# A first norm whose factor is applied to the results of the products, not to their input

## The chip, the cores and the metric

One core of one Trainium2 chip runs the whole program. The metric is the time of one execution on the device, in microseconds (us); the kernel before has a median of 1431.68 us over three runs.

## The reference

One step of a two-layer streaming encoder for 640 frames: 512 of a new stream and 8 x 16 of running streams, 1024 channels each, float32. What matters here is the beginning of layer 0:

```python
def rms_norm(x, g):
    y = xf * lax.rsqrt(jnp.mean(xf * xf, axis=-1, keepdims=True) + EPS)
    return (y * g).astype(x.dtype)

def conv_module(h, hist, g, w_pw1, b_pw1, w_dw, b_dw, ln_g, ln_b, w_pw2, b_pw2):
    a, gate = jnp.split(rms_norm(h, g) @ w_pw1 + b_pw1, 2, axis=-1)
    glu = a * jax.nn.sigmoid(gate)
    full = jnp.concatenate([hist, glu], axis=1)
    y = depthwise_conv(full, w_dw) + b_dw          # 31 taps per channel, causal
    y = jax.nn.silu(layer_norm(y, ln_g, ln_b))
    return h + y @ w_pw2 + b_pw2, full[:, -30:]
```

After it come a feed-forward block, attention, a second feed-forward block and a last norm. They take up the span from about 236 us on and are not touched.

## The kernel before

**Layout.** Channels lie on the 128 partitions: tile `h` is 128 x 8 x 640, eight channel tiles `k` by 640 frames. The frames go in two groups, `g` = 0 and 1, of 320 (`GS`; group 0 holds the 128 frames of the running streams). A float32 product is made of three TensorE products (`mm3`): each operand is split into a rounded part and a rest (`xh`, `xl` for the input, `whi`, `wlo` for weights), and high x high, high x low and low x high are added in PSUM. A split is one activation on ScalarE and one subtraction on VectorE.

**First norm and first products.** `rms(g)` squares the eight tiles of `h` (ScalarE, for group 0 three of them on VectorE), adds them, sums over the partitions with a 128 x 1 product (`colmean`), takes the power -1/2 on GpSimd, and spreads the factor over the partitions with a 128 x 128 product into PSUM (`spread`). Only then `n = h * gain * factor` can be computed (L309), and `xsplit` splits `n` (L190, L192). `glu(c, g)` makes channel tile `c` (0 to 7) of the projection: two PSUM tiles, value and gate, of 24 products each (eight `k` by three). ScalarE reads both with scale and bias (`tanh` at L814, a copy at L817), VectorE multiplies them into `gall` (L823, L830; one half of the channels' `gp`/`gs` views). These two are called the gate below.

**Convolution.** The 31 taps run on three engines: for most channel tiles as products on TensorE (`conv_pe`, L923, after a trip through DRAM that shifts the frames), for channel tiles 0 and 3 of the long stream as scaled copies on ScalarE (`cvt`, L876, four buffers) that GpSimd adds (`ca`, L879), and for the rest as 155 multiply-adds on VectorE (L866, L869: 62 of 512 frames and 93 of 128). When all of `y` is there, `conv_ln(0)` sums it on VectorE (`acc`, L233) and TensorE takes the mean (L243).

**Order.** `PLAN` lists the steps; `a`, `b`, `c`, `C` to `F` are projections. Each step is recorded, and a scheduler lays out each engine's queue by priorities. An engine works its queue off strictly in that order. The PSUM pool `mm0` has four tiles of 128 x 512. Input and weights are read through the queue of SyncE (SP), `vecs` (gains, biases: tile `vec`; tap weights: tile `dwv`) through that of ScalarE. `conv_load` (L890, GpSimd) multiplies `dwv` into a diagonal form for `conv_pe`. `warm(n)` issues products without a use.

Of the kernel before, what the change touches and what calls it, by code (L numbers as in the profile page):

```python
# [15 lines left out]
P = 128  # L16
# [26 lines left out]
WARM_END = 5  # L43
HP = 2000
# [3 lines left out]
PL1 = (0, 2, 0, 0, 0, 0, 0, 0)  # L48
# [7 lines left out]
SSQ = 'avavavaa'  # L56
# [16 lines left out]
WARM = 30, 9, 5, 0  # L73
LNO = ((0, 1, 4, 5, 6, 3, 2, 7), (0, 1, 4, 2, 3, 5, 6, 7))
PLAN = ("a0 y x1 b0 b1 q0 dp1s0 c2 ds1p2 D3 C4 S3 q3 C5 E6 u S4 A4 F6 u k ds2 B4 E7 e S5 A5 F7 f k k k S6 A6 "
# [10 lines left out]
def tile_trunk(ctx, tc, xT, vecs, hist, w_pw1, w_pw2, w_in0, w_out0, w_os0, w_in1, w_out1, w_os1,  # L86
# [36 lines left out]
    load_x(0)  # L123
    vec = cst.tile([P, V_N], F32, name="vec", tag="vec")
    nc.scalar.dma_start(vec, vecs[:, 0:V_N])
    ident = cst.tile([P, P], F32, name="ident", tag="ident")
# [25 lines left out]
    def wsplit(src, k, n, parts=1, pool=0, cuts=1, gains=None, late=False, ties=()):  # L152
        raw = wp.tile([P, 2048], F32, tag="raw", name=nm("raw"))
# [18 lines left out]
        def split():  # L172
            with tc.high_priority(offset=HP):
                for i in range(cuts):
                    a, b = sz * i // cuts, sz * (i + 1) // cuts
                    tie = ties[i] if isinstance(ties, list) else ties
                    with behind(*tie):
                        nc.scalar.activation(out=hi[:, a:b], in_=raw[:, a:b], func=AF.Copy)
                    c = b - (b - a) * pool // 4
                    for eng, a, b in ((nc.vector, a, c), (nc.gpsimd, c, b)):  # L180
                        if a < b:
                            with behind(*tie):
                                eng.tensor_tensor(out=lo[:, a:b], in0=raw[:, a:b],
                                                  in1=hi[:, a:b].bitcast(F32), op=ALU.subtract)
            return hi, lo
# [36 lines left out]
    def colmean(st, pieces, n, cut, tag, eng=nc.gpsimd, accp=None, late=(KT, None)):  # L222
# [17 lines left out]
        for k, f in enumerate(srcs):  # L240
            s = f()
            for t, a in enumerate(tiles(n)):
                mean_end[0] = nc.tensor.matmul(st[:, 512 + t * w + k:513 + t * w + k], s[:, a:a + P],  # L243
                                               onec, start=True, stop=True).ins
# [8 lines left out]
    norm_spread, cover = [None], []  # L253
# [44 lines left out]
    def rms(g, gain, engs=SQ, cut=CUT, eng=nc.gpsimd, hold=None, hook=None):  # L298
        n = gr[g][1]
        bc, _ = rstd_bc([hp(g, k) for k in range(KT)], n, engs, cut, None, eng,  # L300
                        accp=hold and hold(), hook=hook)
        xh, xl = new_xs(g)
        if WARM[2 + g]:
            with behind(norm_spread[0]):
                warm(WARM[2 + g])
        for k in range(KT):
            t = hold() if hold and k < 2 else tp.tile([P, tw[0]], F32, tag="n1", name=nm("n1"),
                                                       bufs=NB1)
            norm_end["n"].append(nc.vector.scalar_tensor_tensor(  # L309
                out=t[:, :n], in0=hp(g, k), scalar=col(gain, k), in1=bc, op0=ALU.mult,  # L310
                op1=ALU.mult).ins)
            xsplit(t[:, :n], xh[:, k, :], xl[:, k, :])
        return xh, xl, None, None
# [464 lines left out]
    pws[1] = wsplit(w_pw1[1], 16, P, cuts=4, pool=PL1[1],  # L778
                    ties=(norm_end["sq"], norm_end["n"][3], norm_end["pow"]))
    load_hist(0, 2)  # L780
    nc.scalar.dma_start(dwv, vecs[:, V_N:])
# [7 lines left out]
    def glu(c, g, wh, wl, mid=None):  # L789
        glu_(c, g, wh, wl, mid)  # L790
        if g == 0:
            nc.sync.dma_start(convs_out[:, c], gs[:, c])

    def glu_(c, g, wh, wl, mid):
        n = gr[g][1]
        ps = []
        for ab in range(2):
            pt = mmt()
            def some(ks):
                return mm3(pt[:, :n], [(wh[:, (ab * 8 + k) * P:(ab * 8 + k + 1) * P],  # L800
                                        wl[:, (ab * 8 + k) * P:(ab * 8 + k + 1) * P])
                                       for k in ks], xk(xs[g], ks), ks[0] == 0, ks[-1] == KT - 1)

            if mid and ab:
                mid(lambda: some(range(0, 4)).ins)
                with tc.issue_after(norm_spread[0]):
                    some(range(4, KT))
            else:
                some(range(KT))
            ps.append(pt[:, :n])  # L810
        with tc.high_priority(offset=HP):
            cover.clear()
            t = tp.tile([P, tw[0]], F32, tag="t1", name=nm("t1"))
            glu_end[0] = nc.scalar.activation(out=t[:, :n], in_=ps[1], func=AF.Tanh, scale=0.5,  # L814
                                              bias=hb1[:, KT + c:KT + c + 1]).ins
# [12 lines left out]
            o = HIST + g * NH - NB * SB * g  # L828
            with behind(*tie):
                gate_end[0] = nc.vector.scalar_tensor_tensor(  # L830
                    out=gp[:, c, o:o + n - ns], in0=t[:, ns:n], scalar=1.0, in1=a[:, ns:n],
                    op0=ALU.add, op1=ALU.mult).ins

# [207 lines left out]
    def step(op, arg):  # L1041
# [11 lines left out]
        elif op == "y":  # L1053
            load_x(1)
        elif op == "x":
            def mid(some):
                def hook():
                    with tc.issue_after(mean_end[0]):
                        cover[:] = [some()]

                with behind(norm_end["xh"][2], norm_end["pow"]):
                    xs[1] = rms(1, V_NCONV, SSQ1, 8, hold=w4t, hook=hook)
            glu(1, 0, *pws[1], mid=mid)
# [813 lines left out]
```

## Time and profile before

| what | us |
|---|---|
| median of 3 runs (lowest, highest) | 1431.68 (1431.62, 1432.91) |
| the profiled execution | 1431.78 |
| its span in the profile | 1430.0 |
| TensorE busy in the span | 1416.8 |
| VectorE, ScalarE, GpSimd busy | 1113.5, 746.9, 278.4 |

In the profile each row of a timeline has start, duration, engine, line, operation, output<-inputs with shapes and a count, and in brackets the idle time before it and what ended that. PE is TensorE, DVE VectorE, ACT ScalarE, POOL GpSimd. A TensorE instruction on float32 without the split (`warm`, sums, spreads) stands there as two.

### The profile page before, as it was taken

To read this page: it belongs to the slowest core of one execution; us is meant where nothing else is said; L and a number is where in the kernel's file an instruction comes from. 1 tells how busy PE (TensorE), PEld (TensorE's weight loads), DVE (VectorE), ACT (ScalarE), POOL (GpSimd) and SP (SyncE) were. 2 spreads that over 40 slices of the span, in tenths; PEclk is the share of its full clock that TensorE was granted. 3 is DMA by queue.
4 is the path that set the end of the run, shared out by engine and by line. 5 is a ranking of instruction groups with operands and counts; after the bars stand their busy time and mean duration, and the time that the engine had idled before them with its cause. 6 is when DMAs were issued, how large, how long until landed. Compare 5 with 4: busy or idle time off the path is not lost.

```text
span 1430.0 us, 28700 instructions
## 1 busy us (share of the span) xinstructions
PE 1416.8 (99%) x11076; PEld 1364.0 (95%) x11076; DVE 1113.5 (78%) x2490; ACT 746.9 (52%) x1633; POOL 278.4 (19%) x335
## 2 busy tenths in 40 slices
PE   9999999999999999999999999999999999999998
PEld 9998799999999999999998998888999999999998
DVE  7799867898888888765666757667898798798765
ACT  5666554554653554545654554544564564464453
POOL 5699121011111110112111111110011111111101
PEclk9999999999999999999999999999999999999999
DMA  7267424154644644524456555561244544554522
GB/s 248 91 176 187 123 84 143 32 122 122 169 107 121 148 115 117 139 89 174 165 185 205 187 179 173 181 218 51 60 108 118 147 125 110 145 131 109 135 72 74
DMA packets 93722, 192.62 MB, mean 135 GB/s; under 512 B 15121, under 2 KB 45585, under 8 KB 90129
## 3 DMA queue, kind: packets, MB, share of 16 engines
q1 hardware_dynamic: 79216, 160.59, 36.0%
q0 software_dynamic: 13504, 29.37, 10.5%
q8 instruction: 87, 1.43, 0.4%
q10 hardware_dynamic: 864, 0.83, 0.2%
q14 instruction: 51, 0.41, 0.1%
HBM read 179.14 MB, written 11.61 MB: 133 GB/s over the span
## 4 chain that ended last, share of the span: by engine, by line
PE 93%; DVE 4%; ACT 1%; issue 1%; DMA 1%; POOL 0%; DVEq 0%; ACTq 0%; POOLq 0%
PE mm L451 52%; PE mm L1311 11%; PE mm L202 6%; PE mm L204 6%; PE mm L203 6%; PE mm L923 3%; PE w L1311 2%; PE am L1484 1%; PE am L1556 1%; PE am L1500 1%; PE w L1455 1%; PE w L1518 1%; PE w L243 1%; PE mm L149 1%; PE w L257 1%
## 5 line engine op out<-in xcount | busy, mean ns | idle before, releaser
L451 PE MATMUL mm<-XH,whi 128*128 128x320 f32 x896 | 275.9, 310 | 1.0 <-ACT t L463 0.7
L451 PE MATMUL mm<-XH,wlo 128*128 128x320 f32 x896 | 276.2, 309 | 0.0
L451 PE MATMUL mm<-XL,whi 128*128 128x320 f32 x896 | 274.7, 309 | 0.0
L375 ACT ACTIVATE whi<-raw 128x512 fp32r<-128x512 f32 (+2 forms) x280 | 167.5, 613 | 148.4 <-PE mm L451 91.9
L376 DVE TENSOR_TENSOR wlo<-raw,whi 128x512 fp32r<-128x512 f32 (+2 forms) x280 | 183.8, 667 | 29.8 <-ACT whi L375 29.2
L451 PE MATMUL mm<-hid,whi 128*128 128x320 f32 x732 | 170.9, 310 | 0.0
L451 PEld LDWEIGHTS mm<-XH,whi 128*128 128x128 f32 x896 | 167.7, 188 | 2.8 <-ACT t L463 1.5
L451 PEld LDWEIGHTS mm<-XH,wlo 128*128 128x128 f32 x896 | 168.2, 188 | 0.0
L451 PEld LDWEIGHTS mm<-XL,whi 128*128 128x128 f32 x896 | 167.7, 188 | 0.0
L202 PE MATMUL mm<-xh,whi 128*128 128x320 f32 (+2 forms) x416 | 128.8, 312 | 0.5 <-DVE h L733 0.4
L203 PE MATMUL mm<-xh,wlo 128*128 128x320 f32 (+2 forms) x416 | 128.0, 309 | 0.0
L204 PE MATMUL mm<-xl,whi 128*128 128x320 f32 (+2 forms) x416 | 125.5, 310 | 1.0 <-DVE xl L192 1.0
L451 PEld LDWEIGHTS mm<-hid,whi 128*128 128x128 f32 x732 | 124.8, 188 | 1.5 <-DVE h L602 0.9
L451 PE MATMUL mm<-hid,wlo 128*128 128x320 f32 x366 | 113.0, 309 | 0.0
L451 PE MATMUL mm<-XH,shi 128*128 128x320 f32 x344 | 106.2, 310 | 1.2 <-DVE h L1588 0.7
L451 PE MATMUL mm<-XH,slo 128*128 128x320 f32 x344 | 106.0, 308 | 0.0
L602 DVE TENSOR_TENSOR h<-h,mm 128x320 f32<-128x320 f32 x168 | 79.1, 482 | 34.2 <-PE mm L451 34.2
L451 PE MATMUL mm<-XL,shi 128*128 128x320 f32 x344 | 105.6, 308 | 0.0
L375 ACT ACTIVATE shi<-raw 128x512 fp32r<-128x512 f32 (+1 forms) x114 | 66.4, 588 | 59.6 <-PE mm L451 31.6
L879 POOL TENSOR_TENSOR ca<-ca,cvt 128x512 f32<-128x512 f32 x60 | 89.5, 1492 | 17.3 <-ACT cvt L876 11.1
L428 POOL DMA_DIRECT2D s<-in_w_in x38 | 22.0, 578 | 309.1 <-ACT shi L375 67.3
L376 DVE TENSOR_TENSOR slo<-raw,shi 128x512 fp32r<-128x512 f32 (+1 forms) x114 | 72.0, 636 | 12.4 <-ACT shi L375 12.0
(337 smaller groups left out, 3663.1 us busy)
## 6 DMA issues: line engine op xcount, KB each, us to landing
raw<-in_w_in SPq DMA_DIRECT2D x152, 256.0 KB
s<-in_w_in POOLq DMA_DIRECT2D x76, 256.0 KB, 4.3
raw<-in_w_os SPq DMA_DIRECT2D x96, 192.0 KB
cache<-in_ck SPq DMA_DIRECT2D x32, 512.0 KB
cache<-in_cv SPq DMA_DIRECT2D x32, 512.0 KB
raw<-in_w_pw SPq DMA_DIRECT2D x11, 1024.0 KB
s<-in_w_os POOLq DMA_DIRECT2D x48, 192.0 KB, 3.6
raw<-in_w_kq SPq DMA_DIRECT2D x8, 1024.0 KB
```

Of the source, the lines that this page charges most:

```text
L149: end = nc.tensor.matmul(pt[:, 0:P], ident, ident, start=True, stop=True)
L202: nc.tensor.matmul(ps, wh, xh, start=(first and i == 0), stop=False)
L203: nc.tensor.matmul(ps, wl, xh, start=False, stop=False)
L204: end = nc.tensor.matmul(ps, wh, xl, start=False, stop=(stop and i == last))
L375: put_end[1] = nc.scalar.activation(out=hi, in_=src, func=AF.Copy).ins
L376: put_end[0] = nc.vector.tensor_tensor(out=lo, in0=src, in1=hi.bitcast(F32), op=sub).ins
L428: nc.gpsimd.dma_start(s1, src[:, 2 * n:3 * n])
L451: last = nc.tensor.matmul(pt, wt, v, start=(first and k == i == 0), stop=(k == n - 1 and i == 2), skip_group_check=True)
L602: hadd[i, u] = [nc.vector.tensor_tensor(out=hv, in0=hv, in1=pt, op=sub if row else add).ins]
L879: nc.gpsimd.tensor_tensor(out=acc, in0=acc, in1=pr, op=ALU.add)
L923: conv_end[0] = nc.tensor.matmul(pt[32 * q:32 * q + 32, 0:n], w4[0:r, 4 * tg + q, :], mv, start=(tg == 0), stop=(tg == 7)).ins
L1311: step_end[0] = nc.tensor.matmul(ps, w, x, start=i == j == 0, stop=i == len(wts) - 1 and j == 2).ins
```

## The change

The first norm's gain is put into the split of `h` itself (`rows`), so the products no longer wait for the factor. The factor times one half is copied to SBUF (`half_rstd`, tile `bc`), and VectorE multiplies it into both PSUM results of every channel tile and group before ScalarE applies `tanh` and bias: 32 new VectorE instructions (L843 and L847 of the changed kernel), while 16 multiplications by gain and factor (L309) go. Input and first weight pieces are issued alternately (`ARRIVE`), `dwv` moves from ScalarE's queue to the end of the inputs on SP's, all squares are on ScalarE, the rest of channel tile 1's weights is split on VectorE alone (`PL1`), and one burst of 24 unused products replaces three of 30, 9 and 5. Channel tiles 0 and 1 run their products in halves of `k`.

```diff
-PL1 = (0, 2, 0, 0, 0, 0, 0, 0)
+AT = 2, 1
+ARRIVE = "x0 x1 w0 w2 x2 x3 w1 w3".split()
+PL1 = (0, 0, 0, 0, 0, 0, 0, 0)
-SSQ = 'avavavaa'
+SSQ = 'aaaaaaaa'
-WARM = 30, 9, 5, 0
+WARM = 24
-PLAN = ("a0 y x1 b0 b1 q0 dp1s0 c2 ...
+PLAN = ("a0 x1 b0 z1 q0 dp1s0 c2 ...
-    load_x(0)
+    for piece in ARRIVE:
+        k = 2 * int(piece[1])
+        if piece[0] == "x":
+            nc.sync.dma_start(h[:, k:k + 2, 0:NH], xT[0][:, k:k + 2, :])
+        else:
+            nc.sync.dma_start(raw0[:, 256 * k:256 * k + 512], w_pw1[0][:, 256 * k:256 * k + 512])
...
+    def rows(g, gain, ks, x):
+        for k in ks:
+            with tc.high_priority(offset=HP):
+                nc.scalar.activation(out=x[0][:, k, :], in_=hp(g, k), func=AF.Copy,
+                                     scale=col(gain, k))
+                nc.vector.scalar_tensor_tensor(out=x[1][:, k, :], in0=hp(g, k),
+                                               scalar=col(gain, k),
+                                               in1=x[0][:, k, :].bitcast(F32), op0=ALU.mult,
+                                               op1=ALU.subtract)
+    def half_rstd(g, engs, eng, hook):
+        bc, _ = rstd_bc([hp(g, k) for k in range(KT)], n, engs, KT, None, eng, hook=hook)
+        b = xp.tile([P, n], F32, tag=f"bc{g}", name=nm("bc"))
+        with tc.high_priority(offset=HP):
+            nc.scalar.activation(out=b, in_=bc, func=AF.Copy, scale=0.5)
+        return b
-    def rms(g, gain, engs=SQ, cut=CUT, eng=nc.gpsimd, hold=None, hook=None):
...
-    with tc.issue_after(warm(WARM[0])), tc.high_priority(offset=2 * HP):
-        xs = [rms(0, V_NCONV, SSQ, SCUT, nc.vector, hook=first), None]
+    xs, bch, evicts = [new_xs(0), new_xs(1)], [None, None], []
+    with tc.issue_after(warm(WARM)):
+        split0 = wsplit(None, 16, P, cuts=4, pool=PL1[0], late=True, raw=raw0)
+        for piece in ARRIVE:
+            i = int(piece[1])
+            if piece[0] == "x":
+                rows(0, V_NCONV, (2 * i, 2 * i + 1), xs[0])
+            else:
+                pws[0] = split0(i)
+    pws[1] = wsplit(w_pw1[1], 16, P, cuts=4, pool=PL1[1])
+    load_x(1)
+    nc.sync.dma_start(dwv, vecs[:, V_N:])
     load_hist(0, 2)
-    nc.scalar.dma_start(dwv, vecs[:, V_N:])
...
-            glu_end[0] = nc.scalar.activation(out=t[:, :n], in_=ps[1], func=AF.Tanh, scale=0.5,
-                                              bias=hb1[:, KT + c:KT + c + 1]).ins
-            nc.scalar.activation(out=a[:, :n], in_=ps[0], func=AF.Identity, scale=0.5,
-                                 bias=hb1[:, c:c + 1])
+                nc.vector.tensor_tensor(out=t[:, :n], in0=pts[1], in1=bch[g], op=ALU.mult)
+                glu_end[0] = nc.scalar.activation(out=t[:, :n], in_=t[:, :n], func=AF.Tanh,
+                                                  bias=hb1[:, KT + c:KT + c + 1]).ins
+                nc.vector.tensor_tensor(out=a[:, :n], in0=pts[0], in1=bch[g], op=ALU.mult)
+                nc.scalar.activation(out=a[:, :n], in_=a[:, :n], func=AF.Identity,
+                                     bias=hb1[:, c:c + 1])
```

The results of channel tiles 0 and 1 of a group stay in PSUM until the group's factor is in SBUF; the list `evicts` holds their readout back. Where before group 0's factor stood ahead of every product, its sum and its spread now stand among the products of channel tile 1 (steps `x` and `z`).

Three places show what the scheduler makes of it. SP's queue from its beginning, before (`in_xa`, `in_xb` are the input of group 0 and 1, `raw` is a weight piece):

```order
L121 DMA h<-in_xa 128x2x320 x4
L164 DMA raw_179<-in_w_pw 128x512 x4
L164 DMA raw_237<-in_w_pw 128x512 x4
L752 DMA gall<-in_hist 128x2x368
L121 DMA h<-in_xb 128x2x320 x4
L752 DMA gall<-in_hist 128x368 x6
```

and changed:

```order
L131 DMA h<-in_xa 128x2x320 x2
L133 DMA raw_76<-in_w_pw 128x512 x2
L131 DMA h<-in_xa 128x2x320 x2
L133 DMA raw_76<-in_w_pw 128x512 x2
L174 DMA raw_166<-in_w_pw 128x512 x4
L123 DMA h<-in_xb 128x2x320 x4
L793 DMA dwv<-in_vecs 128x504
L764 DMA gall<-in_hist 128x2x368
```

`dwv` is now the seventeenth transfer of this queue. GpSimd's queue, before: the end of group 1's sum of squares (`w_38`), its power (L287, `rst_49`; group 0's stands eight sums and splits ahead of it) and `conv_load` (L890):

```order
L233 TENSOR_TENSOR w_38_345<-w_38_345,sq_364 128x320
L233 TENSOR_TENSOR w_38_345<-w_38_345,sq_367 128x320
L287 TENSOR_TENSOR rst_49_375<-rst_373,mhalf 128x3
L890 TENSOR_TENSOR w_117_904<-i_100,dwv 128x1024
L890 TENSOR_TENSOR w_131_1032<-i_100,dwv 128x1024
L890 TENSOR_TENSOR w_162_1242<-i_100,dwv 128x1024
```

and changed, right behind the making of constants (L921 is `conv_load`; `acc_425` is group 1's sum; L298 is the power, `rst_27` that of group 0):

```order
L921 TENSOR_TENSOR w_101_862<-i_105,dwv 128x1024
L921 TENSOR_TENSOR w_115_994<-i_105,dwv 128x1024
L921 TENSOR_TENSOR w_146_1208<-i_105,dwv 128x1024
L243 TENSOR_TENSOR acc_425<-sq_423,sq_426 128x320
L298 TENSOR_TENSOR rst_27_293<-rst_291,mhalf 128x3
L243 TENSOR_TENSOR acc_425<-acc_425,sq_429 128x320
L243 TENSOR_TENSOR acc_425<-acc_425,sq_432 128x320
```

The three `conv_load` steps have moved from behind both powers to a place ahead of both. VectorE's queue where channel tile 1's last results and channel tile 2's first are read and the taps begin, before (`t_68` and `t_110` are gate inputs of channel tiles 1 and 2, L866 and L869 are taps):

```order
L830 SCALAR_TENSOR_TENSOR gall<-t_68_550,t_69_552 128x320
L866 TENSOR_SCALAR w_101_649<-gall,dwv,vec 128x512
L866 TENSOR_SCALAR w_116_840<-gall,dwv,vec 128x128
L866 TENSOR_SCALAR w_101_649<-gall,dwv,vec 128x128
L183 TENSOR_TENSOR wlo_723<-raw_721,whi_722 128x2048
L869 SCALAR_TENSOR_TENSOR w_101_649<-gall,dwv,w_101_649 128x512
L869 SCALAR_TENSOR_TENSOR w_101_649<-gall,dwv,w_101_649 128x128
L823 SCALAR_TENSOR_TENSOR gall<-t_110_778,t_111_780 128x8x16
```

and changed (L843 and L847 are the new multiplications, `mm_409` belongs to channel tile 1, `mm_682` and `mm_683` to channel tile 2; L897 and L900 are taps, L852 a gate):

```order
L843 TENSOR_TENSOR t_52_502<-mm_409,bc_469 128x320
L847 TENSOR_TENSOR t_95_735<-mm_682,bc_310 128x320
L193 TENSOR_TENSOR wlo_677<-raw_675,whi_676 128x2048
L858 SCALAR_TENSOR_TENSOR gall<-t_52_502,t_53_505 128x320
L843 TENSOR_TENSOR t_94_732<-mm_683,bc_310 128x320
L897 TENSOR_SCALAR w_85_603<-gall,dwv,vec 128x512
L897 TENSOR_SCALAR w_100_798<-gall,dwv,vec 128x128
L897 TENSOR_SCALAR w_85_603<-gall,dwv,vec 128x128
L852 SCALAR_TENSOR_TENSOR gall<-t_94_732,t_95_735 128x8x16
```

The first taps now stand behind both new multiplications of channel tile 2.

More of the change, by code (lines that the diff above doesn't have):

```diff
@@ L150, in warm, with wsplit @@
         return end.ins
-    def wsplit(src, k, n, parts=1, pool=0, cuts=1, gains=None, late=False, ties=()):
-        raw = wp.tile([P, 2048], F32, tag="raw", name=nm("raw"))
+    def wsplit(src, k, n, parts=1, pool=0, cuts=1, gains=None, late=False, ties=(), raw=None, order=None):
+        loaded = raw is not None
+        raw = raw or wp.tile([P, 2048], F32, tag="raw", name=nm("raw"))
         hi = wp.tile([P, 2048], F32R, tag="whi", name=nm("whi"))
@@ L791, in glu, with store, flush @@
         if g == 0:
-            nc.sync.dma_start(convs_out[:, c], gs[:, c])
+            def store():
+                nc.sync.dma_start(convs_out[:, c], gs[:, c])
+            evicts.append(store)
+            flush(g)
+    def flush(g):
+        while bch[g] is not None and evicts:
+            evicts.pop(0)()
     def glu_(c, g, wh, wl, mid):
         n = gr[g][1]
[L796 to L810, printed above, removed]
@@ new lines, in some @@
+        def some(ab, ks):
+            return mm3(pts[ab], [(wh[:, (ab * 8 + k) * P:(ab * 8 + k + 1) * P],
+                                  wl[:, (ab * 8 + k) * P:(ab * 8 + k + 1) * P])
+                                 for k in ks], xk(xs[g], ks), ks[0] == 0, ks[-1] == KT - 1).ins
+        if c < 2:
+            parts = [(ab, range(4 * u, 4 * u + 4)) for u in range(2) for ab in range(2)]
+        else:
+            parts = [(ab, range(KT)) for ab in range(2)]
+        if mid:
+            at = mid[0]
+            for part in parts[:at]:
+                end = some(*part)
+            mid[1](end, lambda: some(*parts[at]))
+            with tc.issue_after(norm_spread[0]):
+                for part in parts[at + 1:]:
+                    some(*part)
+        else:
+            for part in parts:
+                some(*part)
@@ L1052, in step, with mid @@
             glu(c, 1, *w)
[L1053 to L1056, printed above, removed]
+        elif op in "xz":
+            g = int(op == "z")
+            def mid(end, more):
                 def hook():
                     with tc.issue_after(mean_end[0]):
[L1059 to L1063, printed above, removed]
+                        cover[:] = [more()]
+                sum_cover[:] = [end]
+                bch[g] = half_rstd(g, (SSQ, SSQ1)[g], (nc.vector, nc.gpsimd)[g], hook)
+                sum_cover.clear()
+                cover.clear()
+            if g == 0:
+                glu(1, 0, *pws[1], mid=(AT[0], mid))
+                rows(1, V_NCONV, range(KT), xs[1])
+            else:
+                glu(1, 1, *pws[1], mid=(AT[1], mid))
         elif op in "CDEF":
```

62 lines of the change are left out of this document (22 added, 40 removed).

## The prediction

> **What bounds the kernel now.** I read the page first, then stretches of time, then the timelines of the beginning. The page:
>
> ```profile
> span 1430.0 us, 28700 instructions
> PE 1416.8 (99%) x11076; PEld 1364.0 (95%) x11076; DVE 1113.5 (78%) x2490; ACT 746.9 (52%) x1633; POOL 278.4 (19%) x335
> PE 93%; DVE 4%; ACT 1%; issue 1%; DMA 1%; POOL 0%; DVEq 0%; ACTq 0%; POOLq 0%
> ```
>
> TensorE is busy for 99% of the span and carries 93% of the chain that ended last. Only what lets TensorE do useful work earlier, or makes it wait, can move the time. The change touches the first 160 us:
>
> ```profile
> core 0: us, PE busy (x) PEld busy (x) DVE busy (x) ACT busy (x) POOL busy (x), PEclk, DMA share, GB/s
> 0.00:15.00 15.00, 13.36 (x100) 13.22 (x100) 8.39 (x18) 8.69 (x15) 5.31 (x18) 1.00 0.89 305
> 15.00:47.00 32.00, 30.95 (x207) 29.77 (x207) 25.31 (x42) 15.80 (x35) 14.06 (x12) 1.00 0.47 141
> 55.40:154.60 99.20, 99.20 (x1115) 93.23 (x1117) 91.41 (x182) 62.85 (x101) 85.47 (x58) 1.00 0.62 166
> ```
>
> For 15 us TensorE is busy with products nobody uses. From 55 to 155 us it never rests, but VectorE is busy 91.41 of 99.20 us: the second bound lies 8% below the first, on the engine that gets 32 new instructions.
>
> ```profile
> 1.64 8.95 PE L149 MATMUL mm<-ident 128*128 128x128 f32 x60 [1.64 <-POOL ident masks.py:199]
> 5.00:6.00 1.00, 1.00 (x7) 1.00 1.05 371
> 6.00:7.00 1.00, 1.00 (x12) 1.00 0.99 339
> 15.07 0.41 PE L202 MATMUL mm<-xh,whi 128*128 128x320 f32 x1
> 27.13 0.72 PE L243 MATMUL w<-onec,w 128*128 128x1 f32 x6
> 37.92 0.70 PE L204 MATMUL mm<-xl,whi 128*128 128x320 f32 x3 [0.46 <-DVE xl L192]
> 46.82 0.46 PE L202 MATMUL mm<-xh,whi 128*128 128x320 f32 x2
> ```
>
> The first useful product starts at 15.07. Channel tiles 0 and 1 need 192; in the program's order 60 are left at 37.92 and channel tile 2 begins at 46.82, so one takes 8.9/60 = 0.148. 192 are 28.4 us; with 1.2 for group 1's sum and spread among them, 2.1 of the 31.75 us are waits. I call the start of channel tile 2 S; before, S = 46.8.
>
> **The start of the products.** The transfers and first steps:
>
> ```profile
> 3.00:18.00 15.00, 14.98 (x114) 14.48 (x113) 11.34 (x25) 9.13 (x19) 4.01 (x5) 1.00 1.05 366
> h<-in_xa SPq DMA_DIRECT2D x4, 320.0 KB
> raw<-in_w_pw SPq DMA_DIRECT2D x8, 256.0 KB
> dwv<-in_vecs ACTq DMA_DIRECT2D x1, 252.0 KB
> 4.28 0.47 ACT L211 ACTIVATE sq<-h 128x320 f32<-128x320 f32 x1 [1.30 <-DMA h<-in_xa]
> 14.55 0.93 ACT L190 ACTIVATE xh<-n 128x320 fp32r<-128x320 f32 x2
> 9.36 2.17 ACT L178 ACTIVATE whi<-raw 128x512 fp32r<-128x512 f32 x4
> 10.06 1.29 DVE L183 TENSOR_TENSOR wlo<-raw,whi 128x512 fp32r<-128x512 f32 x2
> ```
>
> In the changed order ScalarE does two squares, four `xh`, two squares and two `whi` from 4.28 on, when the first input is there: 8 x 0.43 + 0.54 = 8.3 for the first `whi`, 0.65 on VectorE, so the first full product is possible at about 9.1. The second input and weight piece (3 x 320 to 256 KB behind the first, at 366 GB/s under 1 us each) come in time. The 24 unused products are 48 instructions, some 20 at the slow rate of the rows above (7 in a us, until 5.9) and 28 at 12 in a us: they end near 9.0, so they cost nothing. Further on TensorE meets ScalarE's list once: after the second `whi` at 8.8 come six activations of 0.43 and three `whi` of 0.54, the last of them the first of channel tile 1, at 13.0. By 13.2 27 products are issued. 57 more (8.4) and the sum (0.6) lie ahead of the spread, which TensorE reaches at 22.3.
>
> **The factor of group 0.** The spread needs the power on GpSimd, which the new order puts behind three `conv_load` steps and one sum, and those wait for `dwv`.
>
> ```profile
> 28.13 0.90 POOL L287 TENSOR_TENSOR rst<-rst,mhalf 128x3 f32<-128x3 f32 x1 [1.46 <-DVE rst L280]
> 32.83 4.22 POOL L890 TENSOR_TENSOR w<-i,dwv 128x1024 f32<-128x1024 f32 x2 [1.91 <-DVE xl L192]
> 44.77 2.36 DVE L183 TENSOR_TENSOR wlo<-raw,whi 128x1024 fp32r<-128x1024 f32 x2 [0.45 <-ACT whi L178]
> 18.03 0.89 POOL L233 TENSOR_TENSOR w<-sq,sq 128x320 f32<-128x320 f32 x1 [2.52 <-ACT sq L211]
> ```
>
> Ahead of `dwv` and with it SP's queue holds eight inputs of 320 KB, eight weight pieces of 256 and its own 252, with `vec` 5.0 MB: 13.7 us at 366 GB/s from 3 us on, and the first input's row is visible about 0.5 behind its bytes, so 17.3. Then 3 x 2.0 + 0.9 + 1.0 = 7.9: the power at 25.2, the spread at 25.3, TensorE waits 3.0. Without the obstacle nothing waits; if GpSimd's sharing with VectorE is worse than in these rows, 4.5. I take 3.0, since both terms have rows. Then spread 0.6, 12 products to 27.7; the copy of the factor (ScalarE 0.45, behind a square that GpSimd frees at 26.1) and two multiplications free a PSUM tile at 28.0. 96 products of group 1, sum and spread 1.2, and a power that waits on VectorE behind two `wlo` of 1.2 (0.6) end at 44.0. S moves from 46.8 to 44.0: **2.8 us won** (5.8 without the obstacle).
>
> **VectorE from S to the first mean of the layer norm.** TensorE's own work there is the same 110.1 us:
>
> ```profile
> 151.95 2.66 DVE L233 TENSOR_TENSOR acc<-acc,y 128x320 f32<-128x320 f32 x5
> 154.53 2.29 DVE L183 TENSOR_TENSOR wlo<-raw,whi 128x2048 fp32r<-128x2048 f32 x1
> 156.93 0.83 PE L243 MATMUL w<-onec,acc 128*128 128x1 f32 x6
> 158.47 0.17 DVE L247 TENSOR_REDUCE mst<-w 128x3 f32<-128x6 f32 x1 [1.65 <-PE w L243]
> 160.01 3.27 DVE L942 TENSOR_TENSOR y<-y,w 128x320 f32<-128x320 f32 x8 [1.17 <-PE w L257]
> 13.97 1.00 DVE L309 SCALAR_TENSOR_TENSOR n<-h,vec,w 128x320 f32<-128x320 f32 x2 [1.35 <-PE w L257]
> 62.93 0.52 DVE L830 SCALAR_TENSOR_TENSOR gall<-t,t 128x320 f32<-128x320 f32 x1 [1.86 <-ACT t L814]
> 87.90 0.32 DVE L823 SCALAR_TENSOR_TENSOR gall<-t,t 128x128 f32<-128x128 f32 x1 [1.63 <-ACT t L814]
> ACT cvt L876 <- POOL ca L879: 24.5, 36, 2.4
> 86.73 0.72 ACT L876 ACTIVATE cvt<-gall,dwv 128x512 f32<-128x512 f32 x1 [0.65 <-POOL ca L879]
> 87.36 0.51 ACT L814 ACTIVATE t<-mm,hb 128x320 f32<-128x320 f32 x1
> 47.09 48.05 POOL L879 TENSOR_TENSOR ca<-ca,cvt 128x512 f32<-128x512 f32 x30 [10.04 <-ACT cvt L876]
> 50.31 1.44 DVE L866 TENSOR_SCALAR w<-gall,dwv,vec 128x512 f32<-128x512 f32 x3
> ```
>
> `acc` is done at 154.6, 2.3 ahead of TensorE's L243. That slack meets four terms.
> - The three first taps (1.44, at 50.3) and the next 0.6 us of taps now stand behind the multiplications of channel tile 2, whose results end 7.1 us after S: 2.0 later.
> - Of the 32 multiplications 22 come after that. The trace has none with this pair of sources; one from PSUM and SBUF is L942, 3.27/8 = 0.41, and 0.54 is one of L309's shape alone. I take 0.43, near L942, which has operation and shape: 9.5 (bounds 9.0 to 11.9). The ten others and the 16 removed L309 lie ahead of S, where VectorE was idle for 6.7 of 32 us: nothing.
> - VectorE's idle time between 55.4 and 154.6 was 7.8. It ended with ScalarE's `tanh` (rows at 62.93, 87.90), and ScalarE there stands in its queue behind `cvt`, which waits for GpSimd's pace of 1.6 us (24.5 us in all). The new order places most `tanh` behind one more `cvt`, so some waits stay. The gate at 87.90 (S + 41.1), behind the 28th `cvt`, has the 29th there now: a period of 0.65 + 0.72 later, and GpSimd begins 0.5 later after S, since the gate that feeds it has the multiplications ahead: S + 43.0. VectorE, with eight multiplications more ahead and three pairs of taps (0.9 each) fewer, gets there at S + 41.3 and waits 1.7. Four places before it, stepped through alike, give 0.9, 1.3, 1.2 and 0.3; behind it VectorE is later than every `tanh`. 5.4 of idle stay, 2.4 is absorbed.
> - `acc` is late by 2.0 + 9.5 - 2.4 = 9.1, TensorE waits 9.1 - 2.3 = 6.8. The `wlo` of 2.29 in between now lies on the path beside 1.5 of sums, where it had 1.65 to spare: 0.9 more. **7.7 us lost.**
>
> If all idle time were absorbed, the loss would be 9.0 + 2.0 - 7.8 - 2.3 + 0.9 = 1.8; if none, and at 0.54 each, 12.5. A late readout holds a PSUM tile: with four tiles and 24 products (3.5) to each, TensorE stands only when a readout is some 10 late, which 9.1 at the very end just misses, and a wait there would be part of the 6.8. The transfers that follow a late gate (a store and four reads through SP's queue, for the taps on TensorE) run meanwhile. ScalarE does as many readouts as before, GpSimd as many taps. SP's other moved transfers, the history behind `dwv` and channel tile 2's weights behind that, are 2.5 MB more than the 5.0, so there by 25, where 35 would do: nothing. Behind the mean nothing is reordered, so the wait is carried to the end. Sum: 1431.78 - 2.8 + 7.7 = **1436.7 us**; the profiled execution lies 0.1 above the median, and 0.2% (2.9 us) is about what a measurement tells from no change.
>
> **A rule on TensorE's clock.** The rows at 5 and 6 us show the rate changing from 7 to 12 instructions in a us after 4 us of work, with the granted clock printed as 1.00 in both. [...]
>
> **Rivals.**
> - *The two cancel.* For it: VectorE's order is a scheduler's and 7.8 us of idle time were there. If the gates don't wait for GpSimd's pace, the loss is 1.8: 1431.78 - 2.8 + 1.8 = 1430.8, no change. It decides where the absorbed idle time passes 7.3 of the 7.8, since there the loss equals the 2.8 won. Against it: 24.5 us of waits for GpSimd in this stretch.
> - *Faster.* `dwv` lands by 13 us, or GpSimd reaches the power early: no wait at the spread. Then 5.8 is won, and with the loss of 1.8 the time is 1427.8. It decides where the loss stays under 2.9 as well. For it: where `dwv` lands is only estimated, and nothing but the queue's order ties the power to it. Against it: 5.0 MB at 366 GB/s.
> - *Slow restart.* TensorE repeats its start behind the long wait: some 20 instructions at half rate took 4.2 us, of which 2.1 are lost: 1438.8.
>
> **Chances.** VectorE late 0.50, with slow restart 0.10, cancelled 0.20, won 0.20. Slower by over 0.2% 0.60, within 0.20, faster 0.20. The likeliest alone spans 1434.7 to 1440; 8 in 10 needs 1428.5 to 1441.
>
> **What would show it.** First useful product near 9; power at about 25 with `dwv` as what GpSimd waited for; idle at the first spread near 3; S near 44; VectorE busy over 94% from S on; TensorE idle for some 7 us ahead of the 12 sums, released by VectorE's `acc`. I am wrong if `acc` is ahead of TensorE, or if the multiplications take under 0.3.

## The result and the profile after

The changed kernel takes 1441.35 us (median of 6 runs, 1438.68 to 1441.68), the kernel before beside it 1431.65 (median of 6): ratio 1.0063, 95% interval 1.0052 to 1.0075, as the means have it (1440.8 and 1431.8; the medians alone give 1.0068). The direction is the forecast one; the median lies 4.7 above the forecast 1436.7 and just above 1441, where the prediction's wide range ends. The profiled execution took 1438.68 us, 6.9 more than that of before; it is the fastest of the six, and the 2.7 us between it and the median are in no row below. The page:

```profile
span 1436.9 us, 28635 instructions
PE 1415.6 (99%) x11036; PEld 1361.9 (95%) x11036; DVE 1110.1 (77%) x2503; ACT 748.9 (52%) x1638; POOL 276.8 (19%) x331
PE 83%; DVE 7%; POOL 5%; DMA 2%; issue 2%; ACT 1%; SPq 0%; POOLq 0%; DVEq 0%; ACTq 0%
```

TensorE carries 83% of the chain instead of 93%; VectorE, GpSimd and a transfer have taken the rest. TensorE has 40 instructions fewer (20 unused products of two each), which matters further down. Stretches of the changed kernel, columns as in the prediction:

```profile
15.00:47.00 32.00, 26.96 (x177) 26.44 (x176) 12.60 (x27) 12.87 (x27) 15.78 (x12) 0.95 0.55 175
27.70:31.00 3.30, 3.30 (x15) 3.30 (x16) 1.29 (x3) 2.14 (x5) 3.06 (x4) 0.52 0.73 244
47.53:160.96 113.43, 110.73 (x1226) 103.39 (x1224) 103.48 (x212) 72.61 (x115) 94.59 (x62) 1.00 0.54 146
164.20:167.50 3.30, 3.30 (x27) 1.37 (x29) 2.77 (x7) 1.97 (x5) 0.00 (x0) 0.51 0.00 0
```

Two stretches of 3.3 us have half the clock (0.52, 0.51); before, it was 1.00 from its first useful product on. Each begins behind pauses of TensorE. The first, in the timelines of TensorE and GpSimd:

```profile
9.56 0.39 PE L212 MATMUL mm<-xh,whi 128*128 128x320 f32 x1
27.46 1.65 PE L268 MATMUL w<-ident,rst 128*128 128x128 f32 x6 [4.66 <-POOL rst L298]
17.70 8.06 POOL L921 TENSOR_TENSOR w<-i,dwv 128x1024 f32<-128x1024 f32 x3 [15.12 <-DMA dwv<-in_vecs]
25.73 0.85 POOL L243 TENSOR_TENSOR acc<-sq,sq 128x320 f32<-128x320 f32 x1
26.54 0.86 POOL L298 TENSOR_TENSOR rst<-rst,mhalf 128x3 f32<-128x3 f32 x1
```

The first product starts at 9.56 instead of 15.07, and then the group's factor is missing: GpSimd waited for `dwv` until 17.70, worked 8.06 on three `conv_load` steps, and did the power at 26.54. TensorE stood for 4.66, and the six spread instructions then took 1.65 where 0.83 to 0.94 is usual. S is 47.5 (46.8 before): the whole early start is gone. The second, ahead of the first mean of the layer norm (TensorE, then VectorE):

```profile
155.01 2.08 PE L954 MATMUL mm<-xa,w 128*32 128x128 f32 x64 [1.64 <-DMA xa<-sa]
157.30 2.81 PE L954 MATMUL mm<-xa,w 128*32 128x192 f32 x64 [0.20 <-ACT y L869]
161.01 0.83 PE L254 MATMUL w<-onec,acc 128*128 128x1 f32 x6 [0.90 <-DVE acc L243]
163.49 1.20 PE L268 MATMUL w<-ident,mst 128*128 128x128 f32 x6 [0.30 <-DVE mst L968]
160.87 2.28 DVE L193 TENSOR_TENSOR wlo<-raw,whi 128x2048 fp32r<-128x2048 f32 x1
163.07 0.16 DVE L258 TENSOR_REDUCE mst<-w 128x3 f32<-128x6 f32 x1
```

The largest pause, 1.64, is not at the sums: the last gate was late, its trip through DRAM too, and channel tile 7's convolution waited for `xa`. `acc` then held TensorE for 0.90. The reduction starts at 163.07 instead of 158.47. The half clock and one more wait of 0.6 behind it cost 2.1: at the same ScalarE instruction (185.0 before) the changed kernel is 6.7 late, at the end 6.9.

### The profile page after: what moved, and what is told of

Same layout as the page of the kernel before. It is cut to its first block, busy times and chain, and to the rows that moved or that the text cites. A ratio compares the mean times of both kernels' runs of the same rounds, so it can differ in the third digit from the quotient of the medians.

```text
span 1436.9 us, 28635 instructions
## 1 busy us (share of the span) xinstructions
PE 1415.6 (99%) x11036; PEld 1361.9 (95%) x11036; DVE 1110.1 (77%) x2503; ACT 748.9 (52%) x1638; POOL 276.8 (19%) x331
## 3 DMA queue, kind: packets, MB, share of 16 engines
q8 instruction: 86, 1.41, 0.4%
## 4 chain that ended last, share of the span: by engine, by line
PE 83%; DVE 7%; POOL 5%; DMA 2%; issue 2%; ACT 1%; SPq 0%; POOLq 0%; DVEq 0%; ACTq 0%
PE mm L463 51%; PE mm L1349 10%; POOL ca L910 4%; PE mm L212 4%; PE mm L214 4%; PE mm L213 4%; DVE w L900 2%; PE w L1349 2%; PE am L1522 1%; PE am L1594 1%; PE am L1538 1%; PE w L1493 1%; PE w L1556 1%; PE mm L954 1%; POOL w L921 1%
## 5 line engine op out<-in xcount | busy, mean ns | idle before, releaser
L212 PEld LDWEIGHTS mm<-xh,whi 128*128 128x128 f32 x416 | 78.4, 189 | 2.3 <-issue 0.8
```

The source lines that it names most:

```text
L212: nc.tensor.matmul(ps, wh, xh, start=(first and i == 0), stop=False)
```

## The experiments

Theory: two losses with separate causes, the power in GpSimd's queue behind steps that wait for `dwv`, and VectorE's 24 multiplications behind S; the slow clock adds to each. "Late" and "ahead" below compare the start of the same instruction in two traces, this kernel's and that of the kernel before. All edits are to the changed kernel unless another is named.

**e1**: the `conv_load` steps behind group 0's power (`pows` keeps the two powers).

```diff
 def conv_load(c):
-        nc.gpsimd.tensor_tensor(out=w4, ...
+        with behind(pows[0]):
+            nc.gpsimd.tensor_tensor(out=w4, ...
```

> The changed kernel with the three conv_load steps of GpSimd tied behind the power of group 0; dwv is loaded as in the changed kernel. Theory A (queue and VectorE are two separate losses): the power no longer waits for dwv, so the 4.66 us wait at the spread of group 0 and the half-rate instructions behind it (about 1.5) go. S comes from 47.7 to 41.5 to 43.0, VectorE's path from S to the first mean stays 115 us, so TensorE still pauses there, and the time is 4 to 6 us under that of the changed kernel: 1.001 to 1.004 of before. Rival B (group 1 takes the loss over): the conv_load steps now stand ahead of six sums of group 1, which end near 36, so that the second power and spread are late and S moves by under 2 us: ratio 1.004 to 1.006. Rival C (only VectorE's total counts, S does not matter): ratio as for the changed kernel, 1.006.

1437.25 us, ratio 1.0039 (1.0026 to 1.0051). The wait at the first spread is gone, but group 1's sum now waits (TensorE, then what ran ahead of it on GpSimd):

```profile
37.02 0.83 PE L254 MATMUL w<-onec,acc 128*128 128x1 f32 x6 [2.50 <-POOL acc L243]
22.94 5.71 POOL L923 TENSOR_TENSOR w<-i,dwv 128x1024 f32<-128x1024 f32 x3
```

S is 45.2, 2.3 earlier than in the changed kernel. A and B each have a part: 4.66 went, 2.50 came, and half clock stands behind the 2.50 as well (38.1 to 41.5). As A has it, TensorE still pauses ahead of the first mean: 2.43 at 153.5, on VectorE, with half clock from 154.2.

**e2**: no multiplication for channel tiles 2 to 7, so that the factor is left out of them.

```diff
-                nc.vector.tensor_tensor(out=t[:, :n], in0=pts[1], in1=bch[g], op=ALU.mult)
+                if c < 2:
+                    nc.vector.tensor_tensor(out=t[:, :n], in0=pts[1], in1=bch[g], op=ALU.mult)
 (the same for a; ScalarE reads pts with scale=0.5 for c > 1)
```

> The changed kernel without the multiplications of channel tiles 2 to 7 (24 VectorE instructions; ScalarE reads PSUM with scale 0.5, so the factor is left out of these tiles). GpSimd's queue is as in the changed kernel. Theory A: S stays near 47.7 with the wait of 4.66 at the spread, but acc is ahead of TensorE, there is no pause at the first mean and no slow stretch behind it: before plus 1 us (later S) to plus 2, ratio 1.0005 to 1.0015. Rival C (VectorE is not what costs; the wait at the spread alone carries the 7 to 9 us): ratio stays above 1.004. The prediction's own price of 7.7 for VectorE would make it 1431, ratio 0.999 to 1.000.

1434.09 us, ratio 1.0022 (1.0012 to 1.0032). S is 47.4, with 4.92 of wait at the spread; from there to the mean TensorE does not pause and the clock stays 1.00, and at the mean the kernel is 0.73 late, as A has it. `acc` ends at 156.64, S + 109.3 (S + 113.4 with the multiplications): they make it 4.1 later. But 2.1 are lost at the end, so 1.4 between the mean and the end, which no theory had; at 1240.5 TensorE waits 1.02 for a weight.

**e3**: both edits (the factor is left out as in e2).

> Both edits together: power ahead of the conv_load steps, and channel tiles 2 to 7 without the multiplications (factor left out there). Theory A: neither loss is left and the earlier start is kept: S 41.5 to 43.0 against 46.8 before, no pause behind it, 1426.5 to 1428.5, ratio 0.9965 to 0.998. Rival B (group 1's power is late): S near 45, ratio 0.999. Rival D (TensorE is granted a slower clock by the pauses elsewhere, so the gain at S is not carried to the end): ratio 0.999 to 1.001 with S at 42.

1433.93 us, ratio 1.0019 (1.001 to 1.0028), runs from 1431.88 to 1436.61. S is 45.3, as B has it, and D's ratio came, though not by its reason: TensorE passes the mean without a pause, 1.4 earlier than in the kernel before, and the profiled execution (1435.77) is 3.9 late at the end. Of these 5.3, 1.1 go between 243 and 320 us (see e10), 1.7 at one place in a feed-forward block, and 2.5 between 1200 and 1400, where TensorE waits for weights at 1241.4 (1.02) and 1354.0 (0.68). ScalarE, then TensorE, at the first place:

```profile
366.49 0.63 ACT L387 ACTIVATE whi<-raw 128x512 fp32r<-128x512 f32 x1 [4.38 <-DMA raw<-in_w_in]
367.69 0.41 PE L463 MATMUL mm<-XH,whi 128*128 128x320 f32 x1 [1.23 <-ACT whi L387]
```

A weight piece came late. The DMA view of 361.5 to 366.5 (the busy share of the DMA engines in tenths, then one of its queues):

```profile
DMA  9998945595569799997968433100010109666797
q8 instruction: 1, 0.02, 2.0%
```

The last packets dribble in one by one. An instruction fetch of 16 KB is under way from 363.7 to 365.2. By 365.0 all other packets of the weight pieces under way are through, and from 365.2, where the fetch ends, the last ten come one at a time until 366.5; that the fetch held them up is argued from these times alone. In e6 and e11 the same picture stands at the same place (fetch until 373.3 and 365.5, packets one by one until 375.0 and 367.2). Queue q8 moves 1.41 MB in 86 fetches of 16 KB, which is 64 bytes for each of TensorE's 2 x 11036 instructions, so I take it for TensorE's program. In the kernel before, the fetch at that place starts at 357.3, ahead of the transfers. That became theory H, for e9.

**e4**: the kernel before with 24 multiplications by a constant 0.5 (`halves`), ScalarE's scale set to 1.

```diff
+            if c > 1:
+                nc.vector.tensor_tensor(out=t..., in0=ps[1]..., in1=halves..., op=ALU.mult)
 (the same for a and ps[0])
```

> The kernel before with 24 multiplications added on VectorE for channel tiles 2 to 7 (PSUM result times a constant 0.5 in SBUF, where ScalarE then has scale 1): VectorE's new load alone, with the old start and the old GpSimd queue. Theory A: S stays 46.8; 24 x 0.42 = 10 us of VectorE less what idle time and slack take in, as in the changed kernel: acc 3 to 6 us behind TensorE with the slow clock after it, ratio 1.0025 to 1.0045. The prediction's sum (7.7 with 2.0 for late taps) gives 1.005. Rival E (VectorE's idle time absorbs them): ratio under 1.001.

1435.12 us, ratio 1.0025 (1.0015 to 1.0034). TensorE:

```profile
153.77 1.96 PE L936 MATMUL mm<-xa,w 128*32 128x128 f32 x64 [1.29 <-DMA xa<-sa]
157.15 2.82 PE L936 MATMUL mm<-xa,w 128*32 128x192 f32 x64 [1.43 <-ACT y L851]
```

The multiplications alone cost 3.6 us (0.0025 x 1431.3; the medians differ by 3.8), with 2.7 of pauses at channel tile 7's convolution and no slow clock here. The loss is shown without the rest of the change. The runs lie only 1.0 apart, those of e1 to e3 4 to 5.

**e5**: as e1, with `behind(pows[1])`, group 1's power.

> The changed kernel with the conv_load steps tied behind the power of group 1 (in e1 behind that of group 0, where they made the sum of group 1 2.5 us late). Theory A: neither sum waits for them now, S is at 41.5 to 42.5, the pause of TensorE on VectorE's account stays 2 to 3 us, with a slow clock behind it: 1431.5 to 1435.5, ratio 1.000 to 1.003. Rival (an earlier S only lengthens the pause, since VectorE's list decides): as e1, ratio 1.004, with a pause of 5 us.

1435.55 us, ratio 1.0022 (1.0013 to 1.003). S is 40.7, 6.9 earlier than in the changed kernel, from GpSimd's order alone; GpSimd does the power at 21.2. TensorE at the end of the stretch, and its clock behind:

```profile
148.09 5.08 PE L956 MATMUL mm<-xa,w 128*32 128x128 f32 x128 [1.58 <-DMA xa<-sa]
154.46 0.83 PE L254 MATMUL w<-onec,acc 128*128 128x1 f32 x6 [1.29 <-DVE acc L243]
157.10:160.00 2.90, 2.90 (x22) 1.80 (x22) 1.01 (x3) 0.49 (x2) 0.00 (x0) 0.50 0.00 0
```

Two pauses, 2.9 in all, and half clock after them for about 6.8 us. The reduction, at 156.5, is 1.9 ahead of before; at 185 the kernel is 1.0 late. Of the 6.9 won at S against the changed kernel, 6.6 are still there at the mean, against the rival. Another 2.7 are lost by the end.

**e6**: `dwv` back on ScalarE's queue (`nc.scalar.dma_start(dwv, ...)`).

> The changed kernel with dwv back on ScalarE's queue; GpSimd's order is as in the changed kernel. Theory A: dwv is there by 10, the three conv_load steps end by 17, the power of group 0 is ready by 23, no wait at the spread: S at 41.5 to 43 and the time as for e5, ratio 1.000 to 1.003. Rival F (dwv on SP's queue also shifts the later weight transfers, and that is why the runs of the changed kernel and of e1 to e3 lie 3 to 5 us apart, where before and e4 lie 1 to 2 apart): the runs here lie under 1.5 us apart. If the spread of the runs has another cause, they lie 3 us apart or more here too.

1440.72 us, ratio 1.0066 (1.0053 to 1.0078); runs 6.0 apart, so F falls. A failed on S, which is 48.0. GpSimd, VectorE and TensorE:

```profile
5.10 6.34 POOL L921 TENSOR_TENSOR w<-i,dwv 128x1024 f32<-128x1024 f32 x3 [2.53 <-DMA dwv<-in_vecs]
5.40 6.86 DVE L314 SCALAR_TENSOR_TENSOR xl<-h,vec,xh 128x320 fp32r<-128x320 f32 x4
13.91 0.64 PE L213 MATMUL mm<-xh,wlo 128*128 128x320 f32 x1 [4.59 <-DVE wlo L193]
```

`dwv` was early, and the three steps ran while VectorE split the input: four subtractions took 6.86 (1.01 for two further on), `wlo` came late, and TensorE waited 4.59 at 13.91 instead of 4.66 at the spread. The wait moved: with `dwv` early, the steps themselves cause it, beside VectorE.

**e7**: 24 unused products in the wait for group 0's power.

```diff
         if hook:
             hook()
+            if eng is nc.vector:
+                with behind(*cover):
+                    for _ in range(24):
+                        end = nc.tensor.matmul(st[:, 768:896], ident, ident, ...)
+                cover[:] = [end.ins]
```

> The changed kernel with 24 unused products between TensorE's last product before the wait and the spread of group 0 (4.0 us at 12 instructions in a us, into unused columns of the same PSUM tile): the wait for the power stays, but TensorE is not idle in it. Theory G (the idle time itself costs the clock): the six spread instructions take 0.9 instead of 1.65, the products behind them 0.147 each instead of 0.27, granted clock 1.0 from 15 to 45 us; S 1.0 to 1.6 earlier than in the changed kernel, the time 1.0 to 1.6 less. Rival (the slow instructions come from the load on the chip or from the wait for a late operand, not from idling): S and the rows as in the changed kernel.

1438.96 us, ratio 1.0056 (1.0044 to 1.0068), the interval overlapping that of the changed kernel. TensorE:

```profile
22.92 5.52 PE L305 MATMUL w<-ident 128*128 128x128 f32 x48
28.28 0.83 PE L268 MATMUL w<-ident,rst 128*128 128x128 f32 x6
32.71 0.41 PE L212 MATMUL mm<-xh,whi 128*128 128x320 f32 x1 [1.84 <-DVE t L848]
```

G holds for the clock: granted 1.00 from 15 to 45 us, the spread 0.83 instead of 1.65. It gained no time: the 48 instructions start 0.112 apart and took 5.52, not 4.0 (the 12 in a us of the prediction's row counts those that reach over its edges, too), and the copy of the factor stood behind squares that GpSimd's sums let through one at a time (31.7 instead of 29.1), so that TensorE waited 1.84 for a PSUM tile. S is 48.8. Ahead of the first mean TensorE then paused 3.68 at 158.3, and half clock stands from 157.8 to 161.2.

**e8**: e5, with group 0's input multiplied by its factor and split again in place, for channel tiles 2 to 7.

```diff
+    def renorm(g):
+        for k in range(KT):
+            q = tp.tile([P, tw[0]], F32, tag=sqt[0], name=nm("sq"))
+            nc.vector.scalar_tensor_tensor(out=q[:, :n], in0=hp(g, k), scalar=col(V_NCONV, k), in1=bch[g], ...)
+            xsplit(q[:, :n], xs[g][0][:, k, :], xs[g][1][:, k, :])
```

> e5, and group 0's input is normed and split once more in place, as soon as its factor is in SBUF (16 VectorE and 8 ScalarE instructions between 24 and 41 us, where VectorE is idle for two thirds): channel tiles 2 to 7 need no multiplication for group 0, which takes 12 of the 24 off VectorE behind S. Theory A: S 42 to 43, no pause behind it or one under 1 us, the first mean at S + 111.7 as before: 3.5 to 5 earlier than in the kernel before, and 1427 to 1429, ratio 0.997 to 0.9985. Rival D (an earlier start is lost again to late weight transfers further on, as in e3): mean 3.5 to 5 earlier, but ratio 0.999 to 1.001.

1442.85 us, ratio 1.0076 (1.0062 to 1.0091). A fault of the edit: `q` shared the buffers of the squares, group 1's squares stood behind it, and TensorE waited 10.20 for their sum. It says nothing on A or D.

**e9**: the kernel before with `WARM = 20, 3, 1, 0` instead of `30, 9, 5, 0`.

> The kernel before with 24 unused products (20, 3 and 1) instead of 44 (30, 9 and 5), the number that the changed kernel has; a few early loads change places in SP's queue, no computing engine's order changes. In the traces the instruction fetch of TensorE's queue (16 KB every 18 us) stands some 6 to 7 us later against the work in all kernels with 24 unused products than in those with 44, and where a fetch falls on a late weight transfer of the feed-forward block, TensorE waits 0.4 to 1.5 for it (e3, e5 and e6 near 370 us). Theory H (the number of TensorE's instructions ahead, by the place of the fetches, makes the rest of the program 1 to 4 us longer and the runs spread): S as before within 0.5, the runs lie 3 us apart or more, median 1432.5 to 1435, ratio 1.0008 to 1.0025. Rival (the spread has to do with the new start itself): runs within 1.5 of each other, ratio 0.9995 to 1.0005.

1433.49 us, ratio 1.0017 (1.0008 to 1.0026); the runs go from 1431.81 to 1436.84, 5.0 apart, those of before beside them 2.2. H's forecast came: 20 products that nobody uses change the rest of the program. Part of it is early, though. With fewer of them TensorE paused 1.98, 1.00 and 0.72 until its first useful product (15.7) and was granted half clock:

```profile
13.00:15.00 2.00, 2.00 (x8) 1.73 (x8) 0.36 (x1) 1.40 (x3) 2.00 (x4) 0.50 1.07 376
```

In the profiled execution 0.9 of the 1.8 lost is there at 185, the other 0.9 comes later. The fetch near 360, taken at the same work (its time less the kernel's lateness there), starts at 355.9 to 357.3 in before, e4, e7, e10 and e12, which have 44 to 48 unused products, and at 363.4 to 364.1 in the nine others, which have 24. The weight piece of e3's rows was late in e3, e5, e6 and e11 and in none of the five with 44 to 48; in the changed kernel, e1, e2, e8 and e9 a fetch at the same work held up no product. Near 1238 the two sets part wholly: the fetch stands at 1227.7 to 1229.4 and at 1234.7 to 1236.2, and the weight split that follows starts at 1237.3 to 1237.7 and at 1237.9 to 1238.9. That the spread of the runs comes from this too is argued, since one execution of each kernel was profiled.

**e10**: e5 with 20 unused products ahead of channel tile 7's convolution.

```diff
+        if (c, part) == (7, "S"):
+            for _ in range(20):
+                nc.tensor.matmul(pt[:, 0:P], ident, ident, start=True, stop=True)
```

> e5 with 20 unused products ahead of the first products of channel tile 7's convolution, where TensorE waited 1.58 us for a transfer: TensorE's fetches stand as in the kernel before from there on, and part of the wait is filled (20 products take 1.7 us, less what they cover). Theory H: behind the first mean nothing is lost any more (in e5 2.7 of 3.8 us were), runs within 2 us of each other, median 1431.5 to 1433, ratio 1.000 to 1.001. Rival (the losses further on do not depend on it): e5's 1435.5, runs spread over 4 us.

1430.87 us, ratio 0.9996 (0.9987 to 1.0005), runs 1.9 apart. TensorE:

```profile
146.44 4.73 PE L948 MATMUL mm<-ident 128*128 128x128 f32 x40
151.11 4.56 PE L959 MATMUL mm<-xa,w 128*32 128x128 f32 x128
```

4.7 us of useless work took 4.7 us off e5 (1435.55). Ahead of 185 it is 2.35: no pause, no half clock. The rest is behind: at 185 e10 is 1.3 ahead of before, at the end 1.4, where e5 went from 1.0 to 3.8 late. Both parts of H's forecast came, but 1.1 of these 2.75 is not the fetches'. In the feed-forward block from 243 us on, the scheduler laid out ScalarE's and VectorE's queues of e5 in another order. ScalarE in e5, then in e10:

```profile
257.96 0.44 ACT L637 ACTIVATE hid<-w 128x320 f32<-128x320 f32 x1 [1.95 <-PE w L268]
259.02 0.94 ACT L387 ACTIVATE XH<-hid 128x320 fp32r<-128x320 f32 x2 [0.62 <-DVE hid L641]
259.86 0.42 ACT L484 ACTIVATE t<-mm 128x320 f32<-128x320 f32 x1
253.86 0.44 ACT L637 ACTIVATE hid<-w 128x320 f32<-128x320 f32 x1 [1.36 <-PE w L268]
254.91 2.26 ACT L387 ACTIVATE XH<-hid 128x320 fp32r<-128x320 f32 x5 [0.62 <-DVE hid L641]
257.44 0.44 ACT L484 ACTIVATE t<-mm 128x320 f32<-128x320 f32 x1 [0.26 <-PE mm L463]
```

A readout (`t<-mm`) stands behind two splits of `XH` in e5 and behind five in e10. e1, e3, e5, e6 and e11 have the first order, all others that of the kernel before; the five lose 1.1 between 243 and 320 and the others nothing, but for 0.9 in e4. For the fetches 1.6 is left in e5, of which 1.05 falls on the weight near 367.

**e11**: e8 with `q` in the `w4` buffers.

> e8 with the normed tile in another buffer (in e8 it shared the buffers of the squares, so that group 1's squares stood behind the second norming, and TensorE waited 10.2 us for their sum): 12 of the 24 multiplications are off VectorE behind S, and the conv_load steps stand behind the second power. Theory A: S 41.5 to 42.5, pauses ahead of the first mean under 1 us in all, the first mean 3.5 to 5 earlier than in the kernel before; 1427 to 1428.5 if nothing is lost further on, with theory H (24 unused products) 1 to 4 more: ratio 0.997 to 1.0005, runs spread over 3 us. Rival (VectorE's other work only spreads out over the time won): pause of 2 to 3 as in e5, ratio as e5 1.002.

1435.49 us, ratio 1.0019 (1.001 to 1.0028), runs 4.6 apart. Group 1's power came 1.7 late, since on VectorE its input stood behind the second norming and two `wlo` until 36.3, and TensorE still paused 1.98 and 0.93 at channel tile 7, without half clock. It was 1.3 ahead of before at 185 and 4.0 late at the end: 1.1 by the other order of e10's text, 1.70 by one late weight at 368.3, and half clock behind that (370.2 to 373.6). Half of the multiplications less did not remove the pause. With all of them gone there was none in e2 and e3, but there S is 47.4 and 45.3; with an S near 42 it was not tried.

**e12**: e10 with 8 of the 20 in that place and 12 with 32 columns of weights ahead of the sums.

> e10 with its 20 unused products made shorter and put where TensorE waited in e5: 8 of 128 columns ahead of channel tile 7's convolution, 12 with 32 columns of weights ahead of the 12 sums of the first mean. In e10 the 20 took 4.73 us (the text on e10 had 1.7, which is too low: two instructions each, so 40 at 0.118) where e5 waited 1.58, and acc was done 1.2 ahead of TensorE. The count of TensorE's instructions is that of e10. Theory H with theory A: 16 x 0.118 + 24 x 0.036 = 2.8, so 1.9 shorter, of which VectorE's acc (done at 154.4) allows 1.2: the first mean 2.3 to 2.6 earlier than in the kernel before, runs within 2 us, 1428.8 to 1430, ratio 0.998 to 0.999. Rival (a pause of 0.5 to 1.3 in front of the sums is enough for the slow clock, as in e5): 3.4 us of half clock behind the mean, 1.7 lost, ratio 0.9995 to 1.001.

1431.0 us, ratio 0.9998 (0.9989 to 1.0007), runs 2.1 apart. TensorE:

```profile
153.97 2.78 PE L972 MATMUL w<-ident 128*32 128x128 f32 x24
```

An unused instruction takes 0.116 with 32 columns too, so nothing became shorter, and the clock stayed 1.00. The reduction is 0.25 ahead of before instead of 2.3 to 2.6, and TensorE paused 0.80 behind it (170.2), so the forecast 1428.8 to 1430 did not come. e10 and e12 are level with the kernel before; no version here beats it.

## Why the prediction was right, and where it was not

The direction was right, and both mechanisms are shown: e5 removes the first, e2 removes and e4 makes the second. That the sum, +4.9, comes near the +6.9 of the profiled execution is in part luck, since its terms err in both directions: up to S 0.7 lost instead of 2.8 won (3.5 worse), from S to the reduction 3.9 lost instead of 7.7 (3.8 better), and 2.3 behind the reduction, of which the sum had nothing.

- **Start of the products.** 9.56 against 9.1; the 48 unused instructions ended at 9.8. The 7 and 12 in a us are counts of a window's instructions with those at its edges; in the timeline of before, starts are 0.213 apart until 5.84 and 0.112 after it, so the rate nearly doubles there. The clock record of that trace begins at 5.82, so the 1.00 printed for 5 to 6 us says nothing of its first part.
- **Group 0's factor: the mis-sized term.** `dwv` was there at 17.70 (17.3 forecast), but the three steps took 8.06, not 3 x 2.0, beside a VectorE that was splitting. The wait was 4.66 instead of 3.0 (4.5 was named for this case). Behind it came half clock for some 3.4 us, which the likeliest case did not have: six spread instructions at 1.65, products 0.27 apart instead of 0.147. Instead of 2.8 won, 0.7 was lost.
- **VectorE behind S: over-sized.** `acc` ended 5.6 later after S than before (S + 113.4 against S + 107.8), not 9.1. The multiplications were priced right. In e2, where the taps are late as well and the multiplications gone, `acc` ends 1.5 later after S than before, against 2.0 for the taps. Too small was what the rest took in. Groups of VectorE between S and the end of `acc`, the first of before, the others of the changed kernel:

```profile
L183 DVE TENSOR_TENSOR wlo<-raw,whi 128x2048 fp32r<-128x2048 f32 (+1 forms) x8 | 21.5, 2683 | 0.0
L193 DVE TENSOR_TENSOR wlo<-raw,whi 128x2048 fp32r<-128x2048 f32 x7 | 16.4, 2339 | 1.2 <-ACT whi L188 1.2
L843 DVE TENSOR_TENSOR t<-mm,bc 128x320 f32<-128x320 f32 x13 | 6.3, 482 | 0.9 <-PE mm L214 0.9
L847 DVE TENSOR_TENSOR t<-mm,bc 128x320 f32<-128x320 f32 x12 | 5.8, 483 | 3.0 <-PE mm L214 3.0
```

  A multiplication takes 0.48, and the next instruction starts 0.40 behind its start; the prediction's 0.43 lies between. 25 stand behind S; three of them are ahead of the first taps, where VectorE was waiting, so the 22 hold. Idle time fell by only 0.5 (10.5 to 9.95; 2.4 forecast, counted from 55.4). But the seven long `wlo` took 16.4, and in before the same seven, read one by one, 20.3: 3.9 less, which no term had. The busy share from S on is 91%, not over 94%.
- **Where TensorE waits.** The prediction had 6.8 at the sums and the late gate's transfers covered. They were not: 1.64 fell on `xa`, 0.20 on the next piece and 0.90 on the sums. The reduction is 3.9 later after S, not 7.7.
- **"The wait is carried to the end."** In the profiled execution 4.6 at the reduction became 6.7 at 185, by the half clock, and 6.9 at the end. For the other five runs, 1440.1 to 1441.7, it is not shown where the last 1 to 3 us went. The changed kernel has e9's 24 unused products and its fetches stand where e9's do, so late weights as in e3 are likely, but not shown; it was not run with the 20 products of e10.
- **The slow restart**, a rival at 0.10 behind a wait of 6.8, came twice, behind 4.66 and behind pauses of 1.64, 0.20, 0.90 and 0.30. The rival took over the 4.2 us at half rate of the start; the trace shows half clock (0.50) from 27.47 to 30.89 and from 164.01 to 167.42, 3.41 each time, and the 133.12 between are 39 times 3.413 (in e5 it is 6.83). Whether the clock changes in such steps only was not tried, and why pauses of 2.9 in all cost 6.8 us of half clock in e5 and the 2.7 of e4 none is not shown. Idle time alone does not decide: of the 3.41 us ahead of 164.01 TensorE was idle for 0.72, and in e11 pauses of 1.98 and 0.93 had no half clock behind them. How much idle time it takes no run here measured.

## What to carry to other kernels

Before a producer is moved earlier, read the queue of every engine on its path: an instruction that waited 15.12 us for a late transfer held up all behind it here, and three steps in GpSimd's queue were worth 6.9 us of start (e5 against the changed kernel). Price a new load on an engine at 78% by what runs beside it and not by its idle time alone, and follow a late result through its transfers to the first engine that stands. Where TensorE is the bound, its unused products are part of the tuning: 24 of them in a wait went with a granted clock of 1.00 from 15 to 45 us, 0.94 without them (e7), and 20 fewer went with instruction fetches some 7 us later among the weight transfers and a ratio of 1.0017 (e9), so compare variants with the same count. A scheduler can lay out a block far behind the edit anew (1.1 us in five runs here), so compare the queues there as well.

## What the hardware showed that was not expected

- Instruction fetch meets weight transfers. Seven us of shift of TensorE's fetches go with runs 3.0 to 7.3 us apart (nine kernels), against 1.0 to 2.1 in e4, e10 and e12 and up to 3.5 in the kernel before, and with up to 1.6 us between the mean and the end (e5 against e10, the other order taken off). An exception is open: e7, with the fetches of before, has four runs within 1.3 and two 2.6 and 3.7 above their highest. In e3 TensorE's wait of 1.23 at 367.69 ended with a weight's split, not with one of the 86 fetches; the weight piece had landed after one.
- VectorE and GpSimd delay each other. A `wlo` of 128 x 2048, of before and of the changed kernel:

```profile
120.94 2.92 DVE L183 TENSOR_TENSOR wlo<-raw,whi 128x2048 fp32r<-128x2048 f32 x1
121.02 2.29 DVE L193 TENSOR_TENSOR wlo<-raw,whi 128x2048 fp32r<-128x2048 f32 x1
```

  The first started while a `ca` step ran (120.41 to 121.71), the second with GpSimd idle until 121.4. Five of the seven in before took 2.92 to 3.32, all of them beginning during a `ca` step, and the two that began with GpSimd idle 2.43 and 2.29; the more of the step was left, the longer the `wlo`: 0.77 in the row above, 1.18 at 3.32. A `ca` step that begins during a `wlo` takes up to 3.2 instead of 1.3. Why the two slow each other is not shown.
